# A two-layer encoder with four token mixers on one core: weights split three pieces ahead, and the softmax of three mixers turned on VectorE and ScalarE

## The chip, the core and the metric

The kernel runs on one core of a Trainium2 chip. TensorE (PE in the rows) multiplies matrices, VectorE (DVE) and ScalarE (ACT) work element by element, GpSimd (POOL) does a handful of one-column copies here, and SyncE (SP) issues nearly all transfers. Each engine takes its own instructions in order, and waits at an instruction until what it needs is there. The metric is device time in microseconds (us) of one execution; lower is better.

## What is computed

256 tokens of width 2048 pass through two layers and a last RMSNorm. Cut to what matters:

```python
def hybrid_layer(x, ...):
    h = rms_norm(x, norm_g)
    u = jnp.einsum('bsd,de->bse', h, w_in)
    (aq, ak, av, az, bq, bk, bv, bz, cq, ck, cv, cz, dq, dk, dv, dz, gates) = jnp.split(u, IN_OFFSETS, axis=-1)
    ya = banded_attention(...)            # A: window of +-128 tokens, sink logit
    yb = neighbourhood_attention(...)     # B: 2-D window with a learned bias
    yc = dilated_mixture_attention(...)   # C: three dilations, mixed by their denominators
    yd = dense_blocked_attention(...)     # D: dense, q and k RMS-normalised
    y = jnp.stack([ya, yb, yc, yd], axis=2)
    z = jnp.stack([az, bz, cz, dz], axis=2)
    branch = jnp.einsum('bsnm,nmd->bsnd', y * jax.nn.silu(z), w_branch)
    gate = jax.nn.sigmoid(gates.reshape(b, s, N_BRANCH, D_MODEL) + gate_b)
    merged = jnp.sum(gate * branch, axis=2)
    return x + jnp.einsum('bsd,de->bse', merged, w_out)
```

Each mixer has 4 heads of 128 channels. All of it is float32. A softmax row has 256 entries, one per token.

## The kernel before

**Pieces of weight.** All weights lie in HBM as 640 pieces of 128 x 1024 numbers (512 KB), 320 a layer, in the order in which they are used. Piece j is loaded into a tile `raw` (`dma_w`, L112), and then split into two halves (`split_w`, L119): `whi`, the value rounded to TensorE's faster float32 format, which ScalarE writes (L286 in `halves`), and `wlo`, the rest, which VectorE writes after it (L287). A product is made of three matmuls, high by high, high by low and low by high (`mm3`, L213 to L215). With two blocks of 128 tokens and two steps of 128 channels, a piece is worth 12 matmuls of 512 columns.

**The loop.** The main loop (L687 on) takes one piece after the other. At piece j it issues the load of piece j+4 (`LD`), the split of piece j+2 (`LS`), the 12 matmuls of piece j, and then what else is due: one step of the list `post` (turning a finished unit, see below), the evacuation of a unit whose last piece this was (`ev_M`, `ev_gate`, `ev_branch`, `ev_out`), and one slot of the list `side` (attention). `issue_after` keeps that work behind the split of the same turn on ScalarE and VectorE. There are 4 tiles of `raw` and 3 each of `whi` and `wlo`, so a split can begin when TensorE is done with the piece three before it.

**Units.** Eight pieces make a unit of 512 output columns, and two pieces a unit of a mixer's output projection. In a layer the units are, in order: `avdv akdk aq az cv ck dq A0 dz A1 cq0 A2 cq1 A3 cq2 D0 cz D1 bv D2 D3 bk C0 bq bz C1 C2 C3 B0 B1 B2 B3` and four units of `w_out` (`P`). A name like `A0` stands for a gate unit `G` of 8 pieces and a projection `R` of 2. Counted from 0 in the first layer, `ck` is pieces 40 to 47, `dq` 48 to 55, the gate unit of A0 56 to 63.

**Turning a unit.** Projections come out with tokens on the partitions; attention and the next product want channels there. `turn` (L300) lets VectorE transpose the 32 x 32 blocks of a tile in one instruction (L312), and ScalarE then moves 16 blocks of 32 partitions, which it does `step` at a time, one step per piece (L314). `step` is 3 or 4, and 6 for the merged product of B (`ev_branch`) and for the output of a layer (`ev_out`).

**Attention** (`attn_slots`, L407). Each mixer has 8 items, 4 heads by 2 blocks of 128 queries; a slot comes every second piece. An item goes through s1 (scores, TensorE), s2 (mask, maximum, exponential), s3 (division), s4 (TensorE turns the two 128 x 128 parts of the softmax into PSUM, L486) and, once a head's two blocks are there, s5 (the turned softmax is split into `pth` and `ptl`), s6 (product with v, six matmuls into `y`) and s7 (times the SiLU gate, `yz`, split again). Each is one slot behind the one ahead of it. A's slots begin with piece 31, D's with 73, C's with 145, B's with 217.

**The start.** The first pieces, the first parts of x and the tables come through the same queue, SP's. `hold` (L107) makes a load wait for an earlier one by a one-column copy on GpSimd. In the last unit the last pieces go through the first block of tokens alone, and then through the second (`half`, `late`).

Of the kernel before, what the change touches and what calls it, by code (L numbers as in the profile page):

```python
# [17 lines left out]
P = 128  # L18
# [56 lines left out]
def encoder_kernel(ctx: ExitStack, tc: tile.TileContext, a: dict, out: bass.AP):  # L75
    nc = tc.nc
    LD = 4
    LS = 2
    NBUSY = 10

    const = ctx.enter_context(tc.tile_pool(name="const", bufs=1))
# [11 lines left out]
    def nm(s):  # L93
        uid[0] += 1
        return f"{s}_{uid[0]}"
# [15 lines left out]

    def dma_w(j, after=None):  # L112
        if j < NSUB:
            t = wpool.tile([P, 1024], F32, tag="raw", name=nm("raw"))
            hold(t, after)
            nc.sync.dma_start(t, a["w"][j])
            raw_q[j] = t

    def split_w(j):  # L119
        if j < NSUB:  # L120
            raw = raw_q.pop(j)
            hi = wpool.tile([P, 1024], F32R, tag="whi", name=nm("whi"), bufs=3)
            lo = wpool.tile([P, 1024], F32R, tag="wlo", name=nm("wlo"), bufs=3)
            for c in (slice(0, 512), slice(512, 1024)) if j == 0 else (slice(0, 1024),):
                last = halves(raw[:, c], hi[:, c], lo[:, c])
            wstate[j] = (hi, lo)
            return last
        return None
# [12 lines left out]
            nc.sync.dma_start(xT[i], a["x"][:, 2 * i:2 * i + 2, :])  # L141

    nc.sync.dma_start(x0, a["x0"])
    raw_q[0] = wpool.tile([P, 1024], F32, tag="raw", name=nm("raw"))
    for q in range(2):
        c = slice(q * 512, (q + 1) * 512)
        nc.sync.dma_start(raw_q[0][:, c], a["w"][0][:, c])
# [1 line left out]
    dma_x(1, raw_q[0][:, 0:1])  # L149
    dma_w(2, raw_q[0][:, 512:513])  # L150
    dma_x(2, raw_q[1][:, 0:1])
    dma_w(3, xT[1][:, 0, 0:1])
    assert LD == 4
    ones = const.tile([P, P], F32, name="ones")
    nc.vector.memset(ones, 1.0)
    warm = const.tile([P, 1], F32, name="warm")
# [24 lines left out]

    def squares(ss, n, blk):

        s = wk.tile([P, 512], F32, tag="t2", name=nm("sq"))
        nc.scalar.activation(s, xm[n][:, blk, :], AF.Square, accum_out=ss[:, blk, n:n + 1])
        return s

# [142 lines left out]
    def ev_M(layer, name, ps, post):  # L330
        rc = [S["rcq" if name[1] == "q" and name[0] != "d" else "rc"][:, blk:blk + 1] for blk in range(2)]
        x, kind = name[0].upper(), name[1]
        if kind == "v":
            ev_v(ps, {"avdv": "avdv", "bv": "Bv", "cv": "Cv"}[name])
            return
        if name == "bq":
            b_mask()
        u = wk.tile([P, 2, 512], F32, tag="u", name=nm("u"), bufs=1)
        key = x + name[1:]
        for blk in range(2):  # L340
            p, o = ps[:, blk, :], u[:, blk, :]
            if kind == "z":
                s = wk.tile([P, 512], F32, tag="t2", name=nm("zs"))
                nc.scalar.activation(s, p, AF.Sigmoid, scale=rc[blk])
                nc.vector.scalar_tensor_tensor(o, p, rc[blk], s, op0=ALU.mult, op1=ALU.mult)
            elif x == "B":
                nc.scalar.activation(o, p, AF.Copy, scale=rc[blk])
            elif x == "C" or name == "aq":
                rope(p, o, blk, cos1, sin1, rc[blk])
            elif name == "akdk":  # L350
                rope(p[:, 0:256], o[:, 0:256], blk, cos1, sin1, rc[blk])
                d_squares(p[:, 256:512], 4, blk)
                if blk == 0:
                    S["dku"] = per.tile([P, 2, 256], F32, tag="dku", name=nm("dku"))
                rope(p[:, 256:512], S["dku"][:, blk, :], blk, *S["dt"])
            else:
                d_squares(p, 0, blk)
                rope(p, o, blk, *S["dt"])
        if name == "akdk":
            k_pair("A", u[:, :, 0:256], u[:, 0, :], post)  # L360
        elif x == "C" or kind == "z":
            S[key] = st()
            turn(u, S[key], post)
        else:
            S[key + "h"], S[key + "l"] = st(F32R), st(F32R)
# [8 lines left out]
    def d_squares(p, c, blk):  # L374

        n = p.shape[-1] // HD
        if c == 4 and blk == 0:
            S["dv"] = sm.tile([P, 2, 6], F32, tag="dv", name=nm("dv"))
        s = wk.tile([P, 512], F32, tag="t2", name=nm("dsq"))[:, 0:n * HD]
        nc.scalar.activation(s, p, AF.Square)  # L380
        nc.vector.tensor_reduce(S["dv"][:, blk, c:c + n], s.rearrange("p (h d) -> p h d", d=HD), axis=AX.X, op=ALU.add)

# [23 lines left out]
    def attn_slots(x, layer):  # L406
# [19 lines left out]
        def s2(t):  # L426
# [4 lines left out]
            mx = sm.tile([P, 1], F32, tag="mx", name=nm("mx"))  # L431
            ng = sm.tile([P, 1], F32, tag="ng", name=nm("ng"))
            den = sm.tile([P, 1], F32, tag="den", name=nm("den"))
            p = wk.tile([P, 512], F32, tag="p", name=nm("p"), bufs=3)
            if x == "D":
                f = S["fq"][:, blk, h:h + 1]
                nc.vector.tensor_reduce(mx, sc[:, 0:n], axis=AX.X, op=ALU.max)
# [28 lines left out]
        def s3(t):  # L466
# [10 lines left out]
            nc.vector.reciprocal(rd, den)  # L477
            nc.vector.tensor_scalar(p[:, 0:SEQ], p[:, 0:SEQ], rd, None, ALU.mult)

        def s4(t):  # L480
            h, blk = items[t]
            it = I.pop(t)
            if blk == 0:
                H[h] = ps_tp.tile([P, 2, SEQ], F32, tag="tp", name=nm("tp"))
            for k in range(2):
                nc.tensor.transpose(H[h][:, k, blk * P:(blk + 1) * P], it["p"][:, k * P:(k + 1) * P], ident)  # L486

        def s5(h):
            hi = wk.tile([P, 2, SEQ], F32R, tag="pth", name=nm("pth"))
            lo = wk.tile([P, 2, SEQ], F32R, tag="ptl", name=nm("ptl"))  # L490
            halves(H.pop(h), hi, lo)
            H[h] = hi, lo

# [9 lines left out]
        def s7(h):  # L503
# [4 lines left out]
            nc.vector.tensor_tensor(yz, H.pop(h), S[x + "z"][:, h, :], op=ALU.mult)  # L508
            halves(yz, S[x + "yh"][:, h, :], S[x + "yl"][:, h, :])

        n = len(items)
        slots = []
        for t in range(n + 7):
            ops = []
            for lag, fn in ((3, s4), (2, s3), (1, s2), (0, s1)):
                if 0 <= t - lag < n:
                    ops.append((fn, t - lag))
            for lag, fn in ((6, s7), (5, s6), (4, s5)):
                i = t - lag
                if 0 <= i < n and items[i][1] == 1:  # L520
                    ops.append((fn, items[i][0]))
            slots.append(ops)
        return slots

# [29 lines left out]
    def ev_branch(x, n, ps, post):  # L554
# [9 lines left out]
        if x == "B":  # L564

            S[f"mh{n}"], S[f"ml{n}"] = st(F32R), st(F32R)
            turn_split(m, m.rearrange("p b m -> p (b m)"), S[f"mh{n}"], S[f"ml{n}"], post, 6)

    def ev_out(n, ps, post):

# [10 lines left out]
            for c in range(4):  # L581
                h_split(1, 4 * n + c, t[:, c, :])

        turn(xm[n], t, post, split, 6)

    F = {}

# [76 lines left out]
    for layer in range(DEPTH):  # L664
# [3 lines left out]
        for ui, si in sub_list(layer):  # L668
# [30 lines left out]
            nk = 2 * nsub  # L699
            if (name, si) in (("akdk", 5), ("dq", 5)):  # L700
                d_tables(layer, int(name == "akdk"), None if layer or name == "dq" else xm[3][:, 0, 0:1])
            dma_x(j + LD - 1)
            dma_w(j + LD)
            h_tiles(j + LS - 1)
            behind = split_w(j + LS)
            if j in early:
                early[j]()
            if j == 11:
                layer_stats(0, F["ss"])
                ev_M(*held.pop())  # L710
            hi, lo = wstate.pop(j)
            half = alone and si >= 5
            mm_m(outs[:1] if half else outs, hi, lo, sh, sl, 2 * si, nk, j < 4)
            if half:
                late.append((hi, lo, si))
# [154 lines left out]
```

## Time and profile before

| | |
|---|---|
| median of 3 runs | 1863.76 us (1863.42 to 1864.97) |
| the profiled execution's own time | 1864.2 us |
| its span, first to last instruction | 1862.4 us |
| TensorE: matmuls, busy | 8260, 98% of the span |
| VectorE, ScalarE busy | 63%, 62% |
| TensorE's granted clock, mean | 0.998 of 2.4 GHz |
| HBM read | 353 MB |

A matmul's end is modelled and overlaps the next one's start, so "98% busy" does not say that TensorE runs at its best pace. The pace is seen in how many matmuls start in a stretch.

### The profile page before, as it was taken

How to read it: one execution, taken by the hardware profiler on the slowest of the kernel's cores; microseconds unless marked ns; L12 is line 12 of the kernel's file. 1: busy time of each engine (PE TensorE's matmuls, PEld its weight loads, DVE VectorE, ACT ScalarE, POOL GpSimd, SP SyncE). 2: the span in 40 equal slices, each digit the busy share in tenths (PEclk: the TensorE clock that was granted, in tenths of full speed). 3: DMA queues.
4: the chain of work that ended last, by engine and by line, in shares of the span. 5: the costliest groups of instructions: out<-in, count | busy, mean ns of one | idle time of the engine just before them, and what ended most of it. 6: DMA issues, size and time to landing. Idle time of an engine off the chain costs nothing.

```text
span 1862.4 us, 22697 instructions
## 1 busy us (share of the span) xinstructions
PE 1833.5 (98%) x8260; PEld 1505.5 (81%) x8260; DVE 1179.0 (63%) x1600; ACT 1151.7 (62%) x1712; POOL 5.1 (0%) x18
## 2 busy tenths in 40 slices
PE   9999999999999999999999999999999999999998
PEld 7888788888888888777888887888888888887776
DVE  6767566666665675665557675765666556755655
ACT  6676666556446764667767676655575457546663
POOL 1000000000000000000000000000000000000000
PEclk9999999999999999999999999999999999999999
DMA  8655555665576566655665555566655765565754
GB/s 310 203 184 181 180 178 188 198 196 175 183 208 204 180 189 195 197 186 174 190 204 186 177 172 180 175 207 198 196 175 175 220 198 178 189 199 180 222 190 148
DMA packets 110848, 356.94 MB, mean 192 GB/s; under 512 B 19984, under 2 KB 20496, under 8 KB 110736
## 3 DMA queue, kind: packets, MB, share of 16 engines
q1 hardware_dynamic: 110448, 354.98, 60.2%
q8 instruction: 64, 1.05, 0.2%
q10 hardware_dynamic: 288, 0.52, 0.1%
q14 instruction: 48, 0.39, 0.1%
HBM read 353.36 MB, written 2.10 MB: 191 GB/s over the span
## 4 chain that ended last, share of the span: by engine, by line
PE 84%; ACT 9%; DVE 4%; issue 2%; DMA 1%; POOL 0%; DVEq 0%; SPq 0%; ACTq 0%; POOLq 0%
PE ps L214 27%; PE ps L215 27%; PE ps L213 26%; ACT whi L286 2%; DVE wlo L287 2%; ACT u L314 2%; ACT m L314 2%; ACT st L314 1%; PE tp L486 1%; DVE T L312 1%; DVE m L563 0%; ACT dku L314 0%; DMA raw<-w 0%; PE y L214 0%; PE y L213 0%
## 5 line engine op out<-in xcount | busy, mean ns | idle before, releaser
L287 DVE TENSOR_TENSOR wlo<-raw,whi 128x1024 fp32r<-128x1024 f32 (+1 forms) x641 | 779.7, 1220 | 612.1 <-ACT whi L286 609.6
L286 ACT ACTIVATE whi<-raw 128x1024 fp32r<-128x1024 f32 (+1 forms) x641 | 676.4, 1058 | 606.7 <-PE ps L215 486.0
L214 PE MATMUL ps<-wlo,h 128*128 128x512 f32 x2032 | 794.9, 391 | 10.1 <-DVE wlo L287 9.3
L213 PE MATMUL ps<-whi,h 128*128 128x512 f32 x2032 | 794.5, 391 | 2.1 <-ACT whi L286 2.1
L215 PE MATMUL ps<-whi,h 128*128 128x512 f32 x2032 | 791.7, 390 | 0.0
L214 PEld LDWEIGHTS ps<-wlo,h 128*128 128x128 f32 x2032 | 381.7, 188 | 95.6 <-DVE wlo L287 20.7
L213 PEld LDWEIGHTS ps<-whi,h 128*128 128x128 f32 x2032 | 381.7, 188 | 82.4 <-ACT whi L286 5.5
L215 PEld LDWEIGHTS ps<-whi,h 128*128 128x128 f32 x2032 | 381.6, 188 | 78.8
L214 PE MATMUL ps<-wlo,st 128*128 128x512 f32 x512 | 200.8, 392 | 4.6 <-DVE wlo L287 4.6
L213 PE MATMUL ps<-whi,st 128*128 128x512 f32 x512 | 199.8, 391 | 2.2 <-ACT whi L286 2.2
L215 PE MATMUL ps<-whi,st 128*128 128x512 f32 x512 | 199.3, 389 | 0.0
L214 PEld LDWEIGHTS ps<-wlo,st 128*128 128x128 f32 x512 | 96.1, 188 | 28.4 <-DVE wlo L287 8.9
L213 PEld LDWEIGHTS ps<-whi,st 128*128 128x128 f32 x512 | 96.1, 188 | 24.0 <-ACT whi L286 3.9
L215 PEld LDWEIGHTS ps<-whi,st 128*128 128x128 f32 x512 | 96.2, 188 | 19.4
L314 ACT ACTIVATE st<-T 32x256 f32<-32x256 f32 x256 | 106.2, 415 | 7.8 <-DVE T L312 4.1
L314 ACT ACTIVATE u<-T 32x256 f32<-32x256 f32 (+1 forms) x224 | 89.5, 399 | 7.2 <-DVE T L312 4.3
L314 ACT ACTIVATE m<-T 32x256 f32<-32x256 f32 x128 | 53.2, 415 | 10.2 <-DVE T L312 8.7
L549 DVE SCALAR_TENSOR_TENSOR G<-ps,ry,gb 128x512 f32<-128x512 f32 x64 | 45.0, 745 | 12.9 <-PE ps L215 12.8
L551 ACT ACTIVATE G<-G 128x1024 f32<-128x1024 f32 x32 | 34.0, 1061 | 6.9 <-DVE G L549 6.8
L312 DVE STREAM_TRANSPOSE T<-u 128x1024 f32<-128x1024 f32 (+1 forms) x26 | 31.2, 1199 | 7.7 <-ACT dku L314 7.5
L561 DVE TENSOR_TENSOR G<-ps,G 128x512 f32<-128x512 f32 x48 | 30.9, 684 | 5.6 <-PE ps L215 5.6
L459 ACT ACTIVATE p<-p,ng 128x256 f32<-128x256 f32 (+1 forms) x48 | 27.6, 574 | 6.1 <-DVE ng L458 5.2
(141 smaller groups left out, 836.5 us busy)
## 6 DMA issues: line engine op xcount, KB each, us to landing
raw<-w SPq DMA_DIRECT2D x639, 512.0 KB, 3.9
gb<-gate_b SPq DMA_DIRECT2D x32, 256.0 KB, 4.4
xm<-xm SPq DMA_DIRECT2D x4, 512.0 KB, 8.9
st<-rpb SPq DMA_DIRECT2D x32, 64.0 KB, 4.2
st<-x SPq DMA_DIRECT2D x7, 256.0 KB, 6.2
dx<-tabx SPq DMA_DIRECT2D x4, 256.0 KB, 3.9
st<-fg SPq DMA_DIRECT2D x2, 512.0 KB, 5.3
out<-xm SPq DMA_DIRECT2D x4, 256.0 KB, 2.6
```

The costliest lines, as they stand in the source:

```text
L213: nc.tensor.matmul(o, ah, bh, start=start, stop=False)
L214: nc.tensor.matmul(o, ah, bl, start=False, stop=False)
L215: nc.tensor.matmul(o, al, bh, start=False, stop=stop)
L286: return (nc.scalar.activation(hi, u, AF.Copy), nc.vector.tensor_tensor(lo, u, f32(hi), op=ALU.subtract))
L287: nc.vector.tensor_tensor(lo, u, f32(hi), op=ALU.subtract))
L312: nc.vector.transpose(t, u)
L314: nc.scalar.activation(y[c:c + 32, :, :, a:a + 32], x[a:a + 32, :, :, c:c + 32], AF.Copy)
L459: nc.scalar.activation(p[:, 0:n], p[:, 0:n], AF.Exp, bias=ng, scale=1.0, accum_out=den)
L486: nc.tensor.transpose(H[h][:, k, blk * P:(blk + 1) * P], it["p"][:, k * P:(k + 1) * P], ident)
L549: nc.vector.scalar_tensor_tensor(G[:, blk, :], ps[:, blk, :], S["rc"][:, blk:blk + 1], gb, op0=ALU.mult, op1=ALU.add)
L551: nc.scalar.activation(G, G, AF.Sigmoid)
L561: nc.vector.tensor_tensor(o[:, blk, :], ps[:, blk, :], G[:, blk, :], op=ALU.mult)
```

## The change

Weights: `LS` goes from 2 to 3, `whi` and `wlo` get 4 tiles each, and `raw` 3 in place of 4. The first four pieces keep the old distance (`EARLY`); at piece 4 two pieces are loaded and two are split. To make room, some scratch tiles (`t2`, `pth`, `ptl`) have one buffer in place of two.

Softmax: for A, B and D the two blocks of a head lie in one tile, VectorE transposes its 32 x 32 blocks in one instruction (into a tile `tp`, now in SBUF), and 16 moves of 32 partitions bring the blocks to their places: 8 in one slot and 8 in the next, half of each by ScalarE (L501 of the changed file) and half by VectorE (L503). TensorE's two transposes per item go; C keeps them. The slots behind it come one slot later.

Turning: B's merged product and a layer's output are moved 3 blocks at a time in their first three units, 6 only in the last. In the last unit of all, the pieces that go through one block at a time are 4 to 7 in place of 5 to 7.

```diff
-    LS = 2
+    LS = 3
+    EARLY = 4
...
-            t = wpool.tile([P, 1024], F32, tag="raw", name=nm("raw"))
+            t = wpool.tile([P, 1024], F32, tag="raw", name=nm("raw"), bufs=3)
...
-            hi = wpool.tile([P, 1024], F32R, tag="whi", name=nm("whi"), bufs=3)
-            lo = wpool.tile([P, 1024], F32R, tag="wlo", name=nm("wlo"), bufs=3)
+            hi = wpool.tile([P, 1024], F32R, tag="whi", name=nm("whi"))
+            lo = wpool.tile([P, 1024], F32R, tag="wlo", name=nm("wlo"))
...
-    dma_w(3, xT[1][:, 0, 0:1])
-    assert LD == 4
...
+        def turn_p(t, half):
+
+            h, blk = items[t]
+            p = H[h]
+            if half == 0:
+                u = wk.tile([P, 512], F32, tag="tp", name=nm("tp"), bufs=1)
+                nc.vector.transpose(u, p)
+                H[h] = p, u
+            else:
+                p, u = p
+                H[h] = p.rearrange("p (k t) -> p k t", k=2)
+            u = u.rearrange("p (b k d) -> p k b d", b=2, k=2)
+            o = p.rearrange("p (k b t) -> p k b t", b=2, k=2)
+            for c in (0, 32) if half == 0 else (64, 96):
+                for a in range(0, P, 32):
+                    y, z = o[c:c + 32, :, :, a:a + 32], u[a:a + 32, :, :, c:c + 32]
+                    if a < 64:
+                        nc.scalar.activation(y, z, AF.Copy)
+                    else:
+                        nc.vector.tensor_copy(y, z)
...
         def s4(t):
             h, blk = items[t]
             it = I.pop(t)
+            if x != "C":
+                if blk == 1:
+                    turn_p(t, 0)
+                return
...
+        def s4b(t):
+            turn_p(t, 1)
...
-            for lag, fn in ((6, s7), (5, s6), (4, s5)):
+            for lag, fn in ((6, s7), (5, s6), (4, s5)) if x == "C" else ((7, s7), (6, s6), (5, s5), (4, s4b)):
...
-            turn_split(m, m.rearrange("p b m -> p (b m)"), S[f"mh{n}"], S[f"ml{n}"], post, 6)
+            turn_split(m, m.rearrange("p b m -> p (b m)"), S[f"mh{n}"], S[f"ml{n}"], post, 6 if n == 3 else 3)
...
-        turn(xm[n], t, post, split, 6)
+        turn(xm[n], t, post, split, 6 if n == 3 else 3)
...
-            dma_x(j + LD - 1)
-            dma_w(j + LD)
-            h_tiles(j + LS - 1)
-            behind = split_w(j + LS)
+            dma_x(j + 3)
+            h_tiles(j + 1)
+            for k in (1, 0) if j == EARLY else (j < EARLY,):
+                dma_w(j + LD - k, xT[1][:, 0, 0:1] if j == 0 else None)
+                behind = split_w(j + LS - k)
...
-            half = alone and si >= 5
+            half = alone and si >= 4
```

Where instructions stand on an engine is shown at three places. First ScalarE behind the first B projection unit of layer 0 (pieces 260 and 261 are that unit), before the change; `m` is the merged product, and the first `whi` row is the split of piece 261:

```order
L286 ACTIVATE whi_6369<-raw_6315 128x1024
L314 ACTIVATE m_1894<-T_6338 32x8x32 x12
L286 ACTIVATE whi_6393<-raw_6342 128x1024
L314 ACTIVATE m_1894<-T_6338 32x8x32 x4
L286 ACTIVATE whi_6417<-raw_6367 128x1024
L286 ACTIVATE st_6336<-m_1894 128x1024
```

And after it, where the first `whi` row is the split of piece 262:

```order
L285 ACTIVATE whi_6514<-raw_6490 128x1024
L313 ACTIVATE m_1946<-T_6486 32x8x32 x6
L285 ACTIVATE whi_6535<-raw_6512 128x1024
L313 ACTIVATE m_1946<-T_6486 32x8x32 x3
L285 ACTIVATE whi_6556<-raw_6533 128x1024
L313 ACTIVATE m_1946<-T_6486 32x8x32 x3
L285 ACTIVATE whi_6577<-raw_6554 128x1024
L313 ACTIVATE m_1946<-T_6486 32x8x32 x3
```

The moves stand one split later, and 6 of them stand between two splits in place of 12.

Second, ScalarE behind the unit `dq`, before the change: the first row is the split of piece 62, `dku` is D's keys, `u` its queries, `G` A0's gate.

```order
L286 ACTIVATE whi_1764<-raw_1716 128x1024
L314 ACTIVATE dku_543<-T_1654 32x4x32 x16
L286 ACTIVATE whi_1787<-raw_1738 128x1024
L286 ACTIVATE st_1653<-dku_543 128x512
L314 ACTIVATE u_1619<-T_1655 32x8x32 x8
L286 ACTIVATE whi_1809<-raw_1762 128x1024
L314 ACTIVATE u_1619<-T_1655 32x8x32 x4
L286 ACTIVATE whi_1831<-raw_1785 128x1024
L314 ACTIVATE u_1619<-T_1655 32x8x32 x4
L286 ACTIVATE whi_1860<-raw_1807 128x1024
L286 ACTIVATE st_1636<-u_1619 128x1024
```

And after it, where the first row is again the split of piece 62, and `yz` the gated output of A's last head:

```order
L285 ACTIVATE whi_1788<-raw_1764 128x1024
L313 ACTIVATE dku_547<-T_1698 32x4x32 x16
L285 ACTIVATE st_1432<-yz_1810 128x256
L285 ACTIVATE st_1697<-dku_547 128x512
L285 ACTIVATE whi_1816<-raw_1786 128x1024
L285 ACTIVATE whi_1839<-raw_1814 128x1024
L285 ACTIVATE whi_1861<-raw_1837 128x1024
L313 ACTIVATE u_1663<-T_1699 32x8x32 x12
L285 ACTIVATE whi_1883<-raw_1859 128x1024
L313 ACTIVATE u_1663<-T_1699 32x8x32 x4
L285 ACTIVATE whi_1912<-raw_1881 128x1024
L285 ACTIVATE st_1680<-u_1663 128x1024
```

The 16 moves of the keys stand behind the split of the same piece as before, those of the queries one to two splits later, and `yz` has come in between.

Third, SP's queue at the start, before the change (the first row is piece 2, `st` are parts of x):

```order
L116 DMA raw_98<-w 128x1024
L141 DMA st_101<-x 128x512
L116 DMA raw_104<-w 128x1024
L141 DMA st_149<-x 128x512
L116 DMA raw_151<-w 128x1024
```

And after it:

```order
L117 DMA raw_98<-w 128x1024
L142 DMA st_101<-x 128x512
L142 DMA st_146<-x 128x512
L117 DMA raw_152<-w 128x1024
L142 DMA st_172<-x 128x512
```

Part 3 of x now stands ahead of piece 3.

## Rows read from the trace of the kernel before

**Rows 1.** The page's first parts: busy share of TensorE, its granted clock in 40 slices.
```profile
PE 1833.5 (98%) x8260; PEld 1505.5 (81%) x8260; DVE 1179.0 (63%) x1600; ACT 1151.7 (62%) x1712; POOL 5.1 (0%) x18
...
PEclk9999999999999999999999999999999999999999
```

**Rows 2.** Waits, whole run: who waited for whom, us in total, times, longest.
```profile
PE ps L214 <- DVE wlo L287: 13.9, 24, 0.8
PE ps L213 <- ACT whi L286: 4.3, 12, 0.8
```

**Rows 3.** Windows, matmuls of the pieces alone: length, busy (count), clock, DMA share, GB/s.
```profile
544.00:624.00 80.00, 80.00 (x354) 1.00 0.67 205
752.00:860.00 108.00, 103.85 (x448) 1.00 0.60 186
1676.00:1784.00 108.00, 103.85 (x448) 1.00 0.61 193
860.00:960.00 100.00, 97.92 (x424) 1.00 0.60 191
168.00:208.00 40.00, 35.98 (x151) 1.00 0.50 165
1093.00:1133.00 40.00, 35.98 (x151) 1.00 0.53 164
76.00:120.00 44.00, 42.69 (x184) 1.00 0.56 177
336.00:400.00 64.00, 63.75 (x280) 1.00 0.61 192
```

**Rows 4.** Timeline of TensorE: start, duration, line; D's slots without and with transposes.
```profile
223.95 0.39 PE L215 MATMUL ps<-whi,h 128*128 128x512 f32 x1
...
224.53 0.40 PE L213 MATMUL ps<-whi,h 128*128 128x512 f32 x1
...
241.41 0.40 PE L215 MATMUL ps<-whi,h 128*128 128x512 f32 x1
241.65 0.38 PE L486 MATMUL tp<-tab,p 128*128 128x128 f32 x2
...
242.23 0.40 PE L213 MATMUL ps<-whi,h 128*128 128x512 f32 x1
```

**Rows 5.** Lines, shapes apart: count | busy us, mean ns | idle before.
```profile
L287 DVE TENSOR_TENSOR wlo<-raw,whi 128x1024 fp32r<-128x1024 f32 x639 | 778.4, 1222 | 612.0 <-ACT whi L286 609.6
L312 DVE STREAM_TRANSPOSE T<-dku 128x512 f32<-128x512 f32 x2 | 1.4, 703 | 0.0
L260 DVE TENSOR_TENSOR dt<-dx 128x128 f32<-128x128 f32 x8 | 1.9, 284 | 0.0
L168 DVE COPY vec<-st 128x40 f32<-128x40 f32 x1 | 0.2, 184 | 1.3 <-DMA st<-x 1.3
L314 ACT ACTIVATE dku<-T 32x128 f32<-32x128 f32 x32 | 9.8, 307 | 0.4
```

**Rows 6.** Timeline of ScalarE behind `dq`, layer 0.
```profile
182.98 5.09 ACT L314 ACTIVATE dku<-T 32x128 f32<-32x128 f32 x16
...
189.57 3.40 ACT L314 ACTIVATE u<-T 32x256 f32<-32x256 f32 x8
...
200.62 1.28 ACT L551 ACT_TABLE_LOAD   x1
```

**Rows 7.** Windows in A, layer 1: PE, PEld, DVE, ACT, POOL busy (count), clock, DMA.
```profile
1040.00:1060.00 20.00, 20.00 (x99) 16.77 (x99) 15.20 (x35) 13.03 (x24) 0.00 (x0) 1.00 0.63 208
1060.00:1080.00 20.00, 20.00 (x96) 16.59 (x96) 15.38 (x34) 11.26 (x21) 0.00 (x0) 1.00 0.46 146
```

**Rows 8.** The start: SP's and ScalarE's timeline (piece 3), and all loads of pieces.
```profile
9.40 0.33 SPq L116 DMA_DIRECT2D raw<-w  x1
...
14.49 1.06 ACT L286 ACTIVATE whi<-raw 128x1024 fp32r<-128x1024 f32 x1 [0.36 <-DMA raw<-w]
...
DMA to landing us min/median/max: 3.1/3.9/9.0
```

More of the change, by code (lines that the diff above doesn't have):

```diff
@@ L143, in encoder_kernel @@
     nc.sync.dma_start(x0, a["x0"])
-    raw_q[0] = wpool.tile([P, 1024], F32, tag="raw", name=nm("raw"))
+    raw_q[0] = wpool.tile([P, 1024], F32, tag="raw", name=nm("raw"), bufs=3)
     for q in range(2):
@@ L182, in squares @@
     def squares(ss, n, blk):
-        s = wk.tile([P, 512], F32, tag="t2", name=nm("sq"))
+        s = wk.tile([P, 512], F32, tag="t2", name=nm("sq"), bufs=1)
         nc.scalar.activation(s, xm[n][:, blk, :], AF.Square, accum_out=ss[:, blk, n:n + 1])
@@ L342, in ev_M @@
             if kind == "z":
-                s = wk.tile([P, 512], F32, tag="t2", name=nm("zs"))
+                s = wk.tile([P, 512], F32, tag="t2", name=nm("zs"), bufs=1)
                 nc.scalar.activation(s, p, AF.Sigmoid, scale=rc[blk])
@@ L378, in d_squares @@
             S["dv"] = sm.tile([P, 2, 6], F32, tag="dv", name=nm("dv"))
-        s = wk.tile([P, 512], F32, tag="t2", name=nm("dsq"))[:, 0:n * HD]
+        s = wk.tile([P, 512], F32, tag="t2", name=nm("dsq"), bufs=1)[:, 0:n * HD]
         nc.scalar.activation(s, p, AF.Square)
@@ L433, in s2 @@
             den = sm.tile([P, 1], F32, tag="den", name=nm("den"))
-            p = wk.tile([P, 512], F32, tag="p", name=nm("p"), bufs=3)
+            if x == "C" or blk == 0:
+                p = wk.tile([P, 512], F32, tag="p", name=nm("p"), bufs=3)
+                if x != "C":
+                    H[h] = p
+            if x != "C":
+                p = H[h][:, blk * SEQ:(blk + 1) * SEQ]
             if x == "D":
@@ L482, in s4 @@
             it = I.pop(t)
+            if x != "C":
+                if blk == 1:
+                    turn_p(t, 0)
+                return
             if blk == 0:
@@ L488, in s5 @@
         def s5(h):
-            hi = wk.tile([P, 2, SEQ], F32R, tag="pth", name=nm("pth"))
-            lo = wk.tile([P, 2, SEQ], F32R, tag="ptl", name=nm("ptl"))
+            hi = wk.tile([P, 2, SEQ], F32R, tag="pth", name=nm("pth"), bufs=1)
+            lo = wk.tile([P, 2, SEQ], F32R, tag="ptl", name=nm("ptl"), bufs=1)
             halves(H.pop(h), hi, lo)
@@ L509, in s7 @@
             halves(yz, S[x + "yh"][:, h, :], S[x + "yl"][:, h, :])
+        def s4b(t):
+            turn_p(t, 1)
         n = len(items)
         slots = []
-        for t in range(n + 7):
+        for t in range(n + 7 + (x != "C")):
             ops = []
@@ L517, in attn_slots @@
                     ops.append((fn, t - lag))
-            for lag, fn in ((6, s7), (5, s6), (4, s5)):
+            for lag, fn in ((6, s7), (5, s6), (4, s5)) if x == "C" else ((7, s7), (6, s6), (5, s5), (4, s4b)):
                 i = t - lag
                 if 0 <= i < n and items[i][1] == 1:
-                    ops.append((fn, items[i][0]))
+                    ops.append((fn, i if fn is s4b else items[i][0]))
             slots.append(ops)
```

## The prediction

> **What bounds the kernel.** Read the page's busy shares first: TensorE is busy 98% of the span, and its granted clock stays at the full 2.4 GHz in all 40 slices [rows 1]. So the question is at which pace it works. The windows tell: in a stretch without attention or a wait, 354 matmuls of 512 columns show in 80 us [rows 3]; one of them began before the window, so the pace is 80/353 = 0.2266 us each, or 2.72 us for the 12 of a piece. Busy shares hide what the kernel loses, the counts don't. Then the waits: where TensorE stands still, it waits for `wlo` or `whi`, halves of a weight piece, and no other wait counts [rows 2]. Their 18.2 us are idle time alone; a matmul's modelled end covers the start of each gap, so the loss is larger, and I take it from the counts: length less (count - 1) times 0.2266 [rows 3].
>
> - B's four projections: 752 to 860, 447 x 0.2266 = 101.3, lost 6.7 us; the same stretch of layer 1 has the same count: 13.4 together.
> - Layer 0's output units: 860 to 960, 95.9, lost 4.1.
> - Behind `dq`: 168 to 208, 34.0, less 0.7 for six short matmuls of A's last head (about 0.12 each, the step between the three score matmuls that fill the 0.58 us of rows 4, less the 0.23 of a piece's): lost 5.3; layer 1 has the same count: 10.6 together.
> - The rest: 336 to 400 loses 0.8; 76 to 120 has 2.5 us over its pieces, of which five slots of A's scores take 0.35 each (0.58 less 0.23, rows 4) and two pairs of transposes 0.24 each, so 0.3. Taken twice, for both layers: 2.2.
>
> That is 30.3 us of 1864.2 in waits for splits, after the start.
>
> **The change, part by part.** The sum is against the profiled execution's 1864.2 us, which lies 0.4 above the median of the runs.
>
> *Transposes off TensorE.* In a slot of D with scores alone, the time from the last piece matmul before to the first one after is 224.53 - 223.95 = 0.58 us; with a pair of transposes ahead of the same scores it is 242.23 - 241.41 = 0.82 [rows 4]. A pair costs 0.24 us, all of it on the path. Three mixers, 4 heads, 2 blocks and 2 layers make 48 pairs: **-11.5 us**. [...]
>
> *What takes their place.* Per head: one VectorE transpose, 0.70 us; 8 ScalarE moves of 32 x 128, 0.31 each, a form that the keys of D have; and 8 VectorE copies of 32 x 128 that no row shows [rows 5]. They are bounded by a copy of 40 columns, 0.18, and by a sum of 128 columns with two inputs, 0.28; I take 0.24, nearer to the latter, which has the same length. So 2.6 us of VectorE and 2.5 of ScalarE per head, 62 and 60 in all. They are hidden if these engines have the room beside a head's four pieces (10.9 us, with its scores and products about 12.3). The tightest place is A in layer 1: VectorE is busy 30.6 of 40 us [rows 7], and 3.3 heads in that time add 8.6. 39.2 of 40 is just room: I charge **+2** for both layers (0 to +6).
>
> *One more piece of lead.* A split begins when TensorE frees a buffer. Before, that was 2 x 2.72 us ahead of its use, now 3 x 2.72; it takes 1.06 on ScalarE [rows 8] and 1.22 on VectorE [rows 5], so the engines may now be late by 5.9 us in place of 3.2. Whether it helps hangs on where the clumps of other work stand. At B they stand one split later, and are thinner (the first place shown above): at 3.40 us for 8 moves [rows 6], a clump of 12 is 5.1 us and one of 6 is 2.6. B's last unit keeps its step of 6, and its own loss of 6.7/4 = 1.7 is less than the 2.72 gained. The output units' worst clump is of the same kind and lost 4.1 in four units. All of these end: **-13.4 - 4.1 - 2.2 = -19.7**.
>
> *Behind dq it does not help.* The keys' 16 moves stand behind the split of the same piece as before (the second place), since they wait for a chain that starts only when `dq` is done. From there ScalarE works without a break [rows 6]: 5.1 of key moves, 6.8 of query moves (twice 3.4), 1.28 for the gate's table and about as much as a split for its sigmoid, the two copies of keys and queries and the splits of five to six pieces. New ahead of that: A's last heads are one slot later, so `yz` (about 0.4) stands between the moves and the next split, and the moves of A's last two heads (2.5 each) make ScalarE start late on `dq`'s squares. Against it stands one split fewer in the queue of the late part. I walk through the changed order with these durations, from the end of `dq`. The squares start 2.3 late, and after the rotary work the split of piece 59 is done at 10.8, needed at 9.1. The keys are transposed at 15.1, moved at 20.2, and behind them, `yz` and their copy the split of 63 is done at 23.5, needed at 21.6. Twelve moves of the queries end at 29.8, the split of 66 at 32.0, needed at 31.7. Then four moves, a split, the queries' copy and the gate: the split of 68 is done at 39.1, needed at 37.4. Lost 1.7, 1.9, 0.3 and 1.7: 5.6 in place of 5.3 per layer, **+0.6**. Bounds: 2.6 less if the lead counts in full, 3 more if A's moves add to it, in each layer.
>
> *The start.* It is bound by loads: piece 3 is issued at 9.40, and ScalarE waits for it until 14.49 [rows 8]. In the changed queue a 256 KB part of x stands ahead of it (the third place), and from piece 3 on a load waits for a `raw` tile that was split three pieces earlier, not four. 256 KB at the 4.99 us that the 512 KB took would be 2.5 us, at a rate with less in flight under 1; I take **+1** (0 to +3). Later, a tile of `raw` is free 3 x 2.72 - 2.3 = 5.9 us before its split may begin, and a load lands in 3.9 (median) [rows 8]: hidden, and a late one eats lead only.
>
> *The rest at nothing.* Fewer scratch buffers serialise `zs` and `dsq`, beside splits that are early. The last unit's first block may now start its end earlier, but the end is the second block's, which waits for the last matmul.
>
> Sum: 1864.2 - 11.5 + 2 - 19.7 + 0.6 + 1 = **1836.6 us**.
>
> **Rivals.** (1) *The lead helps behind `dq` too*: 2 x 2.6 to 2 x 5.3 less, and the start free: about 1828. For it: TensorE loses there only because ScalarE is late, and one split fewer lies in the way. Against: the place of the key moves. (2) *The lead is eaten in the attention stretches*: the averages of rows 7 hide bursts (a unit's rotary work falls into A and into D), and each of the four stretches, A and D in two layers, gets a stall of 3 us, between the 1.7 of a B unit and the 5.3 behind `dq`: 1837 + 12 = 1849. For it: A's 39.2 of 40 us. Against: 5.9 us of lead swallow a burst of that size, if the next one is far enough. (3) *Slower than before*: the copies of 32 partitions. A head has about 12.3 us of TensorE time; VectorE's busy 30.6 of 40 is 9.4 a head, 0.70 and 8 copies come on top. What is saved is 1864.2 - 1836.6, 27.6 us, plus the 2 charged, over 24 heads 1.2 us. So from (12.3 + 1.2 - 9.4 - 0.7)/8 = 0.43 us a copy on, in all three mixers, the change loses; at 0.6 a head overruns by 9.4 + 0.7 + 4.8 - 12.3 = 2.6, and 1834.6 + 24 x 2.6 is 1897. The nearest rows say 0.28 at most, and ScalarE's moves of the same shape don't suffer. [...] (4) *The distance isn't there*: the scheduler puts the splits where they were. Then only the transposes count: 1864.2 - 11.5 + 2 = 1855. The order at B speaks against it.
>
> **Chances.** Forecast 0.62, rival 1 0.16, rival 2 0.15, rival 3 0.04, rival 4 0.03. The range takes in rival 1 and most of rival 2: 1826 to 1850. A measurement of this kernel can tell 0.2% (3.7 us) from no change. Only rival 3 gives slower, 0.04; within 0.2% lies only its edge, 0.01; faster 0.95.
>
> **What would show it.** Right: 48 pairs of `tp` matmuls gone (32 instructions left, C's); windows over B and over layer 0's output units with the pace 0.2266; waits for `wlo` and `whi` left only at the start and behind `dq`; VectorE busy about 60 us more, ScalarE too; VectorE copies near 0.24. Wrong: waits within A or D, which would be rival 2; no waits behind `dq`, rival 1; a copy over 0.4, rival 3; splits with two pieces of lead, rival 4; or a start over 3 us longer.

## The result and the profile after

The changed kernel takes 1842.99 us (median, 1842.65 to 1843.51), the kernel before 1864.37 beside it: ratio 0.9885, 95% interval [0.9868, 0.9902]. That is 21.4 us less; the forecast was 27.6 less, 1836.6, with a range of 1826 to 1850. The profiled execution took 1843.27, its span is 1841.5.

The page's first parts, which answer to [rows 1]:

```profile
PE 1814.6 (99%) x8164; PEld 1500.9 (82%) x8164; DVE 1237.4 (67%) x1816; ACT 1211.6 (66%) x1904; POOL 5.2 (0%) x18
...
PEclk9999999999999999999999999999999999999999
```

TensorE has 96 instructions fewer, which are the 48 pairs. VectorE is busy 58.4 us more and ScalarE 59.9; 62 and 60 were forecast. Next the waits of TensorE (who waited for whom, us in total, times, longest), which answer to [rows 2]:

```profile
PE y L213 <- DVE ptl L286: 7.4, 12, 1.1
PE ps L212 <- DVE G L581: 3.6, 2, 1.8
PE ps L224 <- ACT whi L285: 2.6, 2, 1.3
PE ps L213 <- DVE wlo L286: 1.5, 2, 0.8
PE ps L212 <- ACT whi L285: 1.3, 2, 0.7
...
PE sc L212 <- ACT p L443: 0.9, 2, 0.4
```

The waits of [rows 2] have shrunk from 36 to a handful, at the start and behind `dq`. At the top stands a wait that the kernel before did not have: the products `y` of the attention wait 12 times for `ptl`, the low half of the turned softmax. Then the windows over B's projections, layer 0's output units and B's projections in layer 1 (matmuls of the pieces alone; length, then busy and count of PE, PEld, VectorE and ScalarE; otherwise as in [rows 3]):

```profile
729.00:837.00 108.00, 108.00 (x478) 89.45 (x477) 10.79 (x16) 0.00 (x0) 1.00 0.63 203
837.00:937.00 100.00, 100.00 (x443) 82.80 (x442) 4.88 (x4) 0.00 (x0) 1.00 0.58 186
1634.00:1742.00 108.00, 108.00 (x478) 89.47 (x477) 10.47 (x16) 0.00 (x0) 1.00 0.65 209
```

477 x 0.2266 is 108.1: no time is lost there any more. So the weight part did its work, and the missing 6 us lie elsewhere. To find them I cut the run into stages of the same pieces in both kernels: a stage is the time from the first matmul of one piece to the first of another, read from TensorE's timeline. Per layer (layer 1: 320 more) A's attention is pieces 32 to 58, behind `dq` 58 to 72, D's 72 to 106, C's 146 to 186, B's 218 to 250, B's projections 250 to 291, the output units 291 to 323 (in layer 1 to the last piece); the start is from the span's beginning to piece 12; "rest" is what is left; the sum ends with the first matmul of the last piece. The table has us for before, both layers added, and for the changed kernel (K) and the twelve experiments below what they differ by. Each column is read from one profiled execution:

| stage | before | K | 1 | 2 | 3 | 4 | 5 | 6 | 7 | 8 | 9 | 10 | 11 | 12 |
|---|---|---|---|---|---|---|---|---|---|---|---|---|---|---|
| start | 41.4 | +1.1 | +0.6 | 0.0 | −0.6 | +2.3 | +0.7 | +0.1 | +1.5 | +2.5 | +0.3 | −0.8 | 0.0 | −0.1 |
| A | 157.4 | 0.0 | −1.0 | +3.5 | 0.0 | +0.2 | −3.2 | +4.1 | −1.1 | −1.1 | −3.1 | −3.1 | −0.6 | 0.0 |
| dq | 86.9 | −0.2 | −5.2 | +2.9 | +0.1 | −2.0 | +0.2 | +0.2 | −4.8 | −10.7 | −7.0 | −7.3 | −10.7 | −8.6 |
| D | 200.8 | −1.3 | +0.1 | +2.4 | +0.1 | −0.9 | −1.2 | +1.2 | −1.1 | −1.1 | −1.1 | −2.9 | −3.2 | −0.1 |
| C | 240.4 | 0.0 | 0.0 | +0.1 | +0.1 | +0.1 | +0.1 | +0.1 | 0.0 | +0.1 | +0.1 | +0.1 | +0.1 | 0.0 |
| B | 189.6 | +0.1 | −0.3 | +0.8 | 0.0 | +0.2 | −4.0 | +0.4 | −4.1 | −4.0 | −3.6 | −4.1 | −4.1 | 0.0 |
| B's proj. | 233.2 | −10.2 | −10.2 | 0.0 | −10.2 | −9.4 | −10.2 | −10.2 | −10.2 | −10.2 | −10.2 | −10.2 | −10.2 | −10.2 |
| output | 169.7 | −6.4 | −5.2 | +0.1 | −3.0 | −0.6 | −6.4 | −6.4 | −6.4 | −6.4 | −6.4 | −6.4 | −6.4 | −3.0 |
| rest | 531.8 | −3.9 | −3.9 | +0.6 | 0.0 | −2.1 | −3.9 | −3.3 | −3.9 | −3.9 | −3.9 | −3.7 | −3.9 | +1.0 |
| sum | 1851.3 | −20.8 | −25.1 | +10.2 | −13.7 | −12.1 | −27.9 | −13.8 | −30.0 | −34.9 | −34.9 | −38.3 | −39.0 | −21.0 |

Column K says where the gain came from: B's projections, the output units and the rest, 20.5 together. A, D and B, from which 48 pairs of transposes went, gained 1.2 in all. `dq` gained 0.2; without a fall of TensorE's clock in layer 1 (last section) it would be about 1.8, an estimate, and run 4, with the same code there, has 2.0.

What happened there, in VectorE's timeline of B, layer 0 (start, duration, line, tile, idle time before):

```profile
670.76 0.93 DVE L503 COPY p<-tp 32x128 f32<-32x128 f32 x4
671.72 2.36 DVE L286 TENSOR_TENSOR wlo<-raw,whi 128x1024 fp32r<-128x1024 f32 x2
673.99 0.70 DVE L490 STREAM_TRANSPOSE tp<-p 128x512 f32<-128x512 f32 x1
674.62 0.12 DVE L481 RECIPROCAL rd<-den 128x1 f32<-128x1 f32 x1
674.66 0.58 DVE L452 CUSTOM_DVE_ANT_1 p<-sc,st 128x256 f32<-128x256 f32 x1
...
675.28 0.91 DVE L503 COPY p<-tp 32x128 f32<-32x128 f32 x4
676.23 0.35 DVE L482 TENSOR_SCALAR p<-p,rd 128x256 f32<-128x256 f32 x1
...
676.56 0.68 DVE L286 TENSOR_TENSOR ptl<-p,pth 128x512 fp32r<-128x512 f32 x1
```

ScalarE's row of the head's `pth`, and TensorE's products beside it:

```profile
672.33 0.61 ACT L285 ACTIVATE pth<-p 128x512 fp32r<-128x512 f32 x1
...
676.32 0.28 PE L212 MATMUL y<-pth,st 128*128 128x256 f32 x1
677.29 0.39 PE L213 MATMUL y<-ptl,st 128*128 128x256 f32 x1 [0.70 <-DVE ptl L286]
677.52 0.28 PE L214 MATMUL y<-pth,st 128*128 128x256 f32 x1
```

The head's last copies end at 671.69 and ScalarE has its `pth` ready at 672.94. But `ptl` is issued at the end of the slot, behind the next head's transpose, mask, copies and scaling, and VectorE comes to it at 676.56. The second product should start 0.12 after the first, the step from the third to the fourth (677.52 to 677.64), and starts 0.97 after it. Over the 12 places such intervals are 9.3 us longer than where nothing waits. VectorE kept to the order of issue: 3.6 us pass between the end of `pth` and the start of `ptl`, while it works off what was issued ahead of it.

### The profile page after: what moved, and what is told of

Same layout as the page of the kernel before. It is cut to its first block, busy times and chain, and to the rows that moved or that the text cites. A ratio compares the mean times of both kernels' runs of the same rounds, so it can differ in the third digit from the quotient of the medians.

```text
span 1841.5 us, 22932 instructions
## 1 busy us (share of the span) xinstructions
PE 1814.6 (99%) x8164; PEld 1500.9 (82%) x8164; DVE 1237.4 (67%) x1816; ACT 1211.6 (66%) x1904; POOL 5.2 (0%) x18
## 4 chain that ended last, share of the span: by engine, by line
PE 81%; DVE 8%; ACT 6%; issue 2%; DMA 2%; SPq 0%; DVEq 0%; POOL 0%; ACTq 0%; POOLq 0%
PE ps L213 26%; PE ps L212 26%; PE ps L214 26%; DVE wlo L286 3%; ACT whi L285 2%; DMA raw<-w 2%; ACT st L313 1%; DVE p L503 1%; DVE T L311 1%; ACT dku L313 1%; DVE tp L490 1%; ACT u L313 0%; DVE G L581 0%; DVE ptl L286 0%; PE sc L416 0%
## 5 line engine op out<-in xcount | busy, mean ns | idle before, releaser
L501 ACT ACTIVATE p<-tp 32x128 f32<-32x128 f32 x192 | 59.1, 308 | 11.3 <-DVE rd L481 7.3
L503 DVE COPY p<-tp 32x128 f32<-32x128 f32 x192 | 42.2, 220 | 3.7
```

The lines of the kernel that those rows point to most:

```text
L501: nc.scalar.activation(y, z, AF.Copy)
L503: nc.vector.tensor_copy(y, z)
```

## The experiments

Each ran with the kernel before beside it on the same chip (medians 1864.79 to 1865.29); ratios carry 95% intervals.

### 1. The weight part alone

All four mixers take C's way through the softmax, by `TE = "ABCD"`; the lead, the steps, the start and the single scratch buffers are the changed kernel's.

```diff
-            if x == "C" or blk == 0:
+            if x in TE or blk == 0:
...
-            if x != "C":
+            if x not in TE:
```

> The weight part of the change (halves three pieces ahead, thinner steps) without the new turn: all 64 pairs of transposes of the four mixers stay on TensorE. Theory 'late halves' (the trace of the changed kernel: the products of A, B and D wait 9.3 us for the low half ptl of the turned softmax, which eats what the 48 pairs gave, 9.0 us by start-to-start intervals): taking both away leaves the time where it is, 1843 +- 2 us, the waits of y for ptl gone and all of the gain over before (about 21) owed to the lead. The prediction's own terms (pairs worth 11.5, new work 2, lead and dq 19.1, start 1) say 1864.4 - 18.1 = 1846. Rival 'the turn is the gain' (lead worth under 12): 1852 or more.

1838.57 us, 0.986 [0.9844, 0.9877]; its runs, 1836.68 to 1840.67, all lie under the changed kernel's. So all of the gain, and more, is the weight part's, and the turn costs about 4. The theory had expected no difference: it knew of the 9.3 us, not of what the turn does behind `dq`. There the weight part alone gains 5.2, with the turn 0.2 (or about 1.8, without the fall of the clock). ScalarE's timeline behind `dq` in this run:

```profile
182.95 5.08 ACT L314 ACTIVATE dku<-T 32x128 f32<-32x128 f32 x16
188.05 1.06 ACT L286 ACTIVATE whi<-raw 128x1024 fp32r<-128x1024 f32 x1
189.02 0.61 ACT L286 ACTIVATE st<-dku 128x512 fp32r<-128x512 f32 x1
189.54 3.39 ACT L314 ACTIVATE u<-T 32x256 f32<-32x256 f32 x8
```

and in the changed kernel, which answers to [rows 6]:

```profile
183.73 5.10 ACT L313 ACTIVATE dku<-T 32x128 f32<-32x128 f32 x16
188.85 0.42 ACT L285 ACTIVATE st<-yz 128x256 fp32r<-128x256 f32 x1
189.18 0.62 ACT L285 ACTIVATE st<-dku 128x512 fp32r<-128x512 f32 x1
189.70 2.94 ACT L285 ACTIVATE whi<-raw 128x1024 fp32r<-128x1024 f32 x3
193.19 5.11 ACT L313 ACTIVATE u<-T 32x256 f32<-32x256 f32 x12 [0.55 <-DVE T L311]
```

Here the split behind the keys ends at 189.11, there the first of the three ends near 190.7, and the queries' moves start 3.65 us later, twelve in a row.

### 2. The turn alone

Lead, buffers of the weight tiles, steps, start and the last unit as before; the scratch tiles keep their one buffer.

```diff
-    LS = 3
-    EARLY = 4
+    LS = 2
...
-            turn_split(m, ..., post, 6 if n == 3 else 3)
+            turn_split(m, ..., post, 6)
```

> The turn of the softmax by VectorE and ScalarE as in the changed kernel, with the weight part, its steps and its start as before (halves two pieces ahead, four raw tiles, three pairs of halves). Theory 'late halves': the pairs give 9.0 and the products' waits for ptl take 9.3 or more, and the splits, only two pieces ahead, are made later by the moves: 1865 to 1875 us, no faster than before. The prediction's terms: 1864.4 - 11.5 + 2 = 1855.

1877.09 us, 1.0064 [1.0049, 1.0079]: slower than before, by 12.3, a little beyond what 'late halves' had. The prediction's terms, 1855, fall. Its waits:

```profile
PE ps L213 <- DVE wlo L286: 20.6, 29, 2.1
PE ps L212 <- ACT whi L285: 8.0, 12, 2.5
PE y L213 <- DVE ptl L286: 3.4, 2, 1.7
```

With two pieces of lead the moves make the weight halves late rather than `ptl`: 28.6 us of such waits, where [rows 2] has 18.2.

### 3. The steps alone

The kernel before, with three moves a piece in `ev_branch` and `ev_out`.

```diff
-            turn_split(m, ..., post, 6)
+            turn_split(m, ..., post, 6 if n == 3 else 3)
...
-        turn(xm[n], t, post, split, 6)
+        turn(xm[n], t, post, split, 6 if n == 3 else 3)
```

> The kernel before with one thing of the change: three moves a piece in place of six for B's and layer 0's output units but the last of four. Theory 'either does' (a clump of 6 moves is 2.6 us, under the 3.2 us by which the engines may be late with two pieces of lead): 6 of the 8 waits of 1.48 us behind B's units go, and most of the 3.9 us of the output units: 1864.4 - 8.9 - 2.5 = 1853 us. Rival 'only the lead' (the split itself and what else stands in the clump still make it late): each unit keeps over half of its wait, 1859 or more.

1851.31 us, 0.993 [0.9915, 0.9945]. 'Either does' holds for B's projections, which gain the full 10.2 without any lead; the output units gain 3.0 of the 6.4 that the whole change brings them.

### 4. The steps of six, with the lead

The changed kernel with the same two lines back at 6.

> The changed kernel with six moves a piece again for all of B's and layer 0's output units. Theory 'the lead is enough' (a clump of twelve moves is 5.1 us, under the 5.9 us by which the engines may be late with three pieces of lead): B's four projections keep the 10.15 us and the output units the 6.4 us that they gained over both layers, 1843 +- 2 us. Rival 'the steps did it' (with the lead of before, three moves a piece alone gave B's projections the same 10.15 us and the output units 3.0): B loses 10 and the output units 3 or more again, 1856 us. Between the two: a unit of twelve moves keeps part of its wait, 1846 to 1852.

1849.86 us, 0.9917 [0.9902, 0.9932], between the two theories. For B the lead is enough (9.4 of 10.2), for the output units it is not (0.6 of 6.4). 100 us of them in layer 0, the matmuls of the pieces alone:

```profile
840.00:940.00 100.00, 98.08 (x425) 78.73 (x424) 4.87 (x4) 0.00 (x0) 1.00 0.56 182
```

425 matmuls where the changed kernel has 443 in the same window. Why a clump of twelve is hidden in B and not here, ScalarE's timeline of this run suggests. Behind B's first unit the split ahead of the clump begins as soon as TensorE frees a tile (so do, with the same lead, those of the changed kernel, at 752.54 and 755.26, each after ScalarE stood idle for 1.66 us). In the output units the splits wait for the load of `raw` instead (ahead of the clump at 888.68 three in a row, by 1.3, 1.6 and 1.0 us), two squares of the new x stand there as well, and so the clump meets less lead. No run shows that this is the cause.

### 5. Halves first

```diff
+            if x != "C":
+                ops.sort(key=lambda o: o[0] is not s5)
             slots.append(ops)
```

> The changed kernel with one thing moved: in a slot of A, B and D the halves pth and ptl of a head are issued ahead of the next head's transpose, moves, scores and exponentials, not behind them. Theory 'order' (ptl is late because it stands in VectorE's queue behind the next head's turn): the waits of y for ptl go from 9.3 to under 2, nothing takes their place, and the time is 1843 - 8 = 1835 us (1833.5 to 1837). Rival 'room' (ScalarE and VectorE have no time for 2.5 us of moves a head beside the splits, as the prediction's charge and its second rival have it): the loss turns up again as waits for wlo or whi within A, B and D, and less than 3 us are gained: 1840 or more.

1836.43 us, 0.9849 [0.9834, 0.9864], 6.6 under the changed kernel; 'order' is confirmed. `ptl` comes ahead of the next head's turn:

```profile
670.71 2.36 DVE L286 TENSOR_TENSOR wlo<-raw,whi 128x1024 fp32r<-128x1024 f32 x2
672.99 0.69 DVE L286 TENSOR_TENSOR ptl<-p,pth 128x512 fp32r<-128x512 f32 x1
673.59 0.70 DVE L490 STREAM_TRANSPOSE tp<-p 128x512 f32<-128x512 f32 x1
```

The waits of `y` fall from 7.4 to 1.0, B gains 4.0 and A 3.2. D does not move: its scores wait, which the waits of this run show:

```profile
PE sc L212 <- ACT p L443: 1.3, 4, 0.4
...
PE y L213 <- DVE ptl L286: 1.0, 2, 0.6
```

### 6. All moves on VectorE

Halves first, and

```diff
-                    if a < 64:
-                        nc.scalar.activation(y, z, AF.Copy)
-                    else:
-                        nc.vector.tensor_copy(y, z)
+                    nc.vector.tensor_copy(y, z)
```

> Halves first, and all 16 moves of a head of A, B and D on VectorE, none on ScalarE. Theory 'ScalarE is what is late' (behind dq and in D, where the scores wait for the exponential that frees their bank): ScalarE is relieved of 2.5 us a head, VectorE gets 8 copies of 0.22 more; dq goes from +1.7 to about -4 over both layers, D gains 2: 1836.4 - 7 = 1829 us. Rival 'VectorE has no room': per head of A 9.4 of other work, 0.7 and 3.5 are 13.6 us against 12.3 of TensorE, 1.3 a head in eight heads of A and part of it in D and B: 1836.4 + 10 = 1846 us or more.

1850.78 us, 0.9923 [0.9906, 0.9939]: the rival is right. ScalarE is relieved, and yet:

```profile
PE ps L213 <- DVE wlo L286: 10.2, 11, 2.1
PE ps L212 <- DVE G L580: 4.1, 2, 2.1
```

So VectorE does have an edge, at 3.5 us of copies a head (16 at the changed kernel's 0.220): A, D and B lose about 14 us against run 5, though the kernel stays faster than before. With half of the copies it does not reach it.

### 7. Only B and D turned

Halves first, and A's transposes on TensorE again (`TE` as in 1).

```diff
+    TE = "AC"
...
-            if x == "C" or blk == 0:
+            if x in TE or blk == 0:
...
+            if x not in TE:
+                ops.sort(key=lambda o: o[0] is not s5)
```

> Halves ahead of the next head's turn as before this run, and A's softmax turned by TensorE again (its moves gone from ScalarE and VectorE), B's and D's as in the changed kernel. By stages of the runs so far the lead alone gains 5.2 us behind dq in both layers, and with the turn this is 1.7 lost; the turn gives A 3.6, B 3.7 and D 1.3. Theory 'A's moves spoil dq' (A's last heads are moved while dq's squares, keys and queries want ScalarE): dq gains its 5.2 again, A gives back 3.6, so 1836.4 - 6.9 + 3.6 = 1833 us (1832 to 1835). Rival 'the order or D's own turn spoils it': dq stays at +1.7, 1840 us.

1834.02 us, 0.9832 [0.9817, 0.9846], as 'A's moves spoil dq' expected. `dq` is at −4.8 again, A gives back 2.2: A's turn gave less than it cost behind `dq`.

### 8. The moves behind dq shared

As 7, and every second move of D's keys and queries goes to VectorE (`both` is passed from `ev_M`, for D alone).

```diff
-                nc.scalar.activation(y[c:c + 32, :, :, a:a + 32], x[a:a + 32, :, :, c:c + 32], AF.Copy)
+                o, i = y[c:c + 32, :, :, a:a + 32], x[a:a + 32, :, :, c:c + 32]
+                if both and a % 64:
+                    nc.vector.tensor_copy(o, i)
+                else:
+                    nc.scalar.activation(o, i, AF.Copy)
```

> The kernel with B's and D's softmax turned, halves first, and in addition half of the 32 moves behind dq (keys and queries of D) on VectorE, which stands idle 4 us twice there. Theory 'ScalarE's chain behind dq': it is shorter by 8 x 0.31 + 8 x 0.42 = 5.9 us a layer, and the 2.6 us a layer that are still lost there with the lead go: 1833 - 5 = 1828 us (1827 to 1830). Rival 'VectorE or the loads set it' (the splits there wait for raw tiles too, and the copies stand ahead of wlo): under 2 us gained, 1831 or more.

1828.42 us, 0.9802 [0.9787, 0.9816]. `dq` gains 10.7, which is the 10.6 that [rows 3] had as lost there. What is left of TensorE's waits, beside the start:

```profile
PE sc L212 <- ACT p L448: 1.3, 4, 0.4
```

### 9. A turned too

As 8, with A, B and D turned (the lines against the changed kernel; the shared moves of 8 are not shown again).

```diff
-                k_pair("D", S["dku"], S["dku"].rearrange("p b m -> p (b m)"), post, 4)
+                k_pair("D", S["dku"], S["dku"].rearrange("p b m -> p (b m)"), post, 4, True)
...
+            if x != "C":
+                ops.sort(key=lambda o: o[0] is not s5)
```

> The changed kernel (A, B and D turned) with halves first and half of the 32 moves behind dq on VectorE. Theory 'A's moves cost only behind dq' (there ScalarE is late; with its chain 5.9 us shorter there is room): A keeps the 3.6 us that its pairs give and dq stays near -10 over both layers: 1828.4 - 3.6 = 1825 us (1823.5 to 1826.5). Rival 'A's last heads still come in the way': dq falls back by as much as it did without the sharing (6.8), at -4, and A's turn costs more than it gives: 1828.4 - 3.6 + 6.8 = 1831.6.

1828.75 us, 0.9808 [0.9793, 0.9823], the same time as without A and between the theories: A gains 2.0, `dq` loses 3.7.

### 10 and 11. The exponential first in D

In D's slots `s2`, which frees the scores' bank, goes ahead of the next head's turn too: 10 on top of 9, 11 on top of 8.

```diff
-                ops.sort(key=lambda o: o[0] is not s5)
+                ops.sort(key=lambda o: (o[0] is not s5) + (x != "D" or o[0] is not s2))
```

> As the run with A, B and D turned and the shared moves, and in D's slots the exponential of the scores also issued ahead of the next head's transpose and moves. Theory 'D's scores wait for the bank that the exponential frees' (sc after the exponential of D is the one new wait in D, 4 times; D's stage gained 0.6 us a layer in place of 8 x 0.23 = 1.9): the wait goes and D gains 1.2 a layer: 2.4 us under the run without it. Rival 'the records' waits are a shift of others': under 1 us.

> As the run with B and D turned and the shared moves (1828.4), and in D's slots the exponential ahead of the next head's transpose and moves: by the same theory 1828.4 - 2.4 = 1826 us, D's stage at -3.6 over both layers in place of -1.15; by the rival 1827.5 or more.

1826.86 us (0.9799 [0.9783, 0.9815]) and 1825.07 us (0.9786 [0.9772, 0.9801]). D's stage gains 1.8 and 2.1 of the 2.4 that were expected, and the wait of `sc` is gone. Run 11 is the fastest of all, 17.9 us under the changed kernel; its waits are

```profile
PE ps L224 <- ACT whi L286: 1.6, 2, 1.3
PE busy L166 <- DVE ones L154: 1.1, 1, 1.1
PE tp L520 <- DVE p L487: 0.2, 1, 0.2
```

and only the first two, both of the start, are worth a word.

### 12. Thin clumps, no lead

The kernel before with the edits of 3 and the shared moves of 8.

> The kernel before (two pieces of lead, all transposes on TensorE) with the thinner steps of the change and half of the 32 moves behind dq on VectorE: the clumps thinned, no lead added. Before's steps alone gave 1851.3. Theory 'the clump is what counts' (a lead only covers it): dq gains most of the 10.7 us that it gained with lead and shared moves, 9 or more, 1842 us or less, and the lead is worth what is left in the small waits and the output units, about 8 us. Rival 'dq needs the lead too' (16 moves in a clump are still 2.5 us on each engine beside splits of 1.06 and 1.22 with only 3.2 us to spare): dq gains under 5, 1846 us or more.

1842.98 us, 0.9883 [0.9866, 0.9899]: the time of the changed kernel, without its lead and without its turn. 'The clump is what counts' for B's projections and for 8.6 of the 10.7 behind `dq` (9 or more had been expected, and 1842 or less). What column 8 has more in stages without attention stands for the lead, though its kernel also has B and D turned: 3.4 in the output units, 2.2 behind `dq`, and 4.9 in what the table calls rest. Without a turn on either side and without sharing, run 1 is 12.7 us under run 3: that is the lead on top of the thinner steps.

## Why the prediction was near, and which step failed

- **The bound** was read rightly: TensorE at 0.2266 a matmul, losing time only where a weight half is late. In run 11 little else is left.
- **One more piece of lead, −19.7.** Measured −20.5 (B's projections and output units 16.6 for 17.5, small ones 3.9 for 2.2). The size was right, the reason only in part. At B the thinner clump by itself does all of it (run 3), the lead by itself nearly all (run 4), and the change has both; the output units need both. That 5.9 us of lead hide a clump of 5.1 held for B, not for the output units, whose lead is spent in part before the clump comes (run 4).
- **Transposes off TensorE, −11.5.** The price of 0.24 a pair was about right: once nothing waits, B and D gain 3.7 and 3.3 over the lead alone (runs 11 and 1), 0.23 and 0.21 for each of 16 pairs. In A the transposes do better on TensorE, since the turn gains 2.0 there and loses 3.7 behind `dq` (run 9 against run 8; run 7 agrees); in B they do not, the turn gives 3.7.
- **What takes their place, +2 (0 to +6): this is the step that failed.** A, D and B gained 1.2, 1.3 of it by the lead: the turn gave nothing there, so its new work cost all that the pairs are worth, 10 to 11 us, and 3 to 5 more behind `dq` (below). I priced it by busy time ("39.2 of 40 is just room"), and by that there was room: two windows in A, layer 1, hold 17.2 and 17.3 of 20 us.

```profile
1036.00:1056.00 20.00, 20.00 (x97) 16.82 (x96) 17.18 (x43) 14.91 (x33) 0.00 (x0) 1.00 0.57 185
1044.00:1064.00 20.00, 19.73 (x94) 16.30 (x93) 17.34 (x45) 14.23 (x34) 0.00 (x0) 1.00 0.44 138
```

  These two overlap, and lie later in A than those of [rows 7]. The stretch of [rows 7], now 1026.6 to 1066.6, holds 35.9 of 40, less than the 39.2 forecast; its fullest 20 us, 1030 to 1050, hold 19.2, and no piece and no product waits in them. The prices of single instructions were right as well (answering to [rows 5]):

```profile
L501 ACT ACTIVATE p<-tp 32x128 f32<-32x128 f32 x192 | 59.1, 308 | 11.3 <-DVE rd L481 7.3 <-DVE tp L490 0.9 <-DVE den L475 0.8
L503 DVE COPY p<-tp 32x128 f32<-32x128 f32 x192 | 42.2, 220 | 3.7
L490 DVE STREAM_TRANSPOSE tp<-p 128x512 f32<-128x512 f32 x24 | 16.9, 705 | 0.0
```

  0.220 for the copy that I took at 0.24. What I left out is the place of `ptl` in VectorE's queue: behind the next head's turn, and two pieces later TensorE wants it. Run 5 puts it ahead and gets 6.6 us back, with the same two windows as full (17.3 and 17.4). The place of D's exponential, behind the same moves, was worth 2 more (runs 10 and 11).
- **Behind dq, +0.6.** Measured −0.2, by an estimate −1.8 without the fall of the clock: near by luck more than by the walk. Of its four waits those of pieces 59 and 63 came (0.3 and 1.9 for 1.7 and 1.9), at 66 stood 2.0 for 0.3, and there it was not a split but the bank that VectorE's gate `G` gave back late, queued behind a `wlo` that had itself waited 4.0 us for ScalarE's twelve moves and the `whi` behind them; the wait at 68 did not come. And "the lead does not help behind `dq`" is wrong as put, by the place of the keys' moves: alone it gains 5.2 there. It is A's turn that takes them back (run 7, where `dq` gains 4.8 again), which the walk had as "New ahead of that": the gain that it denied and this cost came near to cancelling.
- **The start, +1.** Measured +1.1. Kernels with this same start show −0.8 to +2.5, so a hit there says little.
- **The rivals.** Rival 1 is true of the lead without the turn. Rival 2 had most of the place and nearly the size (12 us in A and D) but not the mechanism: the lead was not eaten, no piece waits within A or D; the products do, and in B as much as in A. Rival 3, slower than before, did not come, its copy being 0.220; that VectorE has an edge is so, and it lies between 8 and 16 copies a head (run 6). Rival 4 is out, though B alone would not show it, since run 3 loses nothing there either: with the third piece of lead, run 1 is 12.7 us under run 3.

## What to carry to other kernels

When work moves from the engine that sets the pace to one with idle time, ask of each result where its instruction stands in the new engine's queue and when it is wanted, not only whether there is busy time left: the same instructions in another order were 6.6 us apart here. Look at a burst that makes a stream late before buying buffers against it: thinning it and sharing it between two engines gave here, without any buffer, as much as the whole change (run 12). And a change of two parts wants both tried alone: here one part gave more than the whole.

## What the runs showed that I had not expected

Behind `dq` in layer 1 of the changed kernel the granted clock fell. The windows, in the columns of [rows 7]:

```profile
1108.00:1112.00 4.00, 3.20 (x15) 2.31 (x13) 1.66 (x2) 3.89 (x8) 0.00 (x0) 1.00 0.38 124
1112.00:1114.00 2.00, 0.97 (x4) 0.87 (x5) 1.75 (x3) 1.98 (x3) 0.00 (x0) 0.94 0.71 195
1114.00:1116.00 2.00, 2.00 (x7) 1.54 (x6) 1.49 (x2) 1.97 (x3) 0.00 (x0) 0.50 0.85 201
1116.00:1118.00 2.00, 2.00 (x8) 1.60 (x7) 0.61 (x1) 2.00 (x3) 0.00 (x0) 0.70 0.65 238
1118.00:1122.00 4.00, 4.00 (x19) 3.29 (x18) 4.00 (x5) 1.38 (x2) 0.00 (x0) 1.00 0.41 149
```

After TensorE had stood still for 1.8 us, eight matmuls ran at half the clock (0.50 from 1114 to 1116), 0.43 us apart in place of 0.2266, and the next ones at the full clock again (1.00 from 1118): about 1.6 us on top of the wait, an estimate from eight times the difference. In layer 0 the same wait, 1.8 us too, had no such fall; this is why layer 1 loses 1.35 us more there. The page's row of 40 slices, at 9 throughout, does not show it.

Five of the other profiled executions have such stretches of six to nine matmuls at 0.43 us: run 2 (in A and behind `dq`; its mean clock is 0.997), run 3 (behind `dq`, 0.52 from 195 to 197), runs 4 and 8 (at the start, from 18 to 22: 0.55 and 0.59, 0.61 and 0.54) and run 6 (in A, 0.50 from 156 to 158). They can add up to 1.8 us (an estimate: nine times 0.20) to a stage of the table, but need not: in run 3 the fall at piece 64 cost nothing, since the wait at piece 67, 1.5 us in layer 1, was gone after it.
